# One DMA queue in place of two: whole 32 KB rows, and loads and stores in turn, in a contrast kernel

## The chip, the cores and the metric

The kernel runs on one core of a Trainium2 chip. The metric is the device time of one execution in microseconds, as the median of the runs. The profile's span, from the first to the last instruction, is a little shorter.

## The reference

The input is a batch of 16 images with 3 channels of 512 x 512 pixels in float32, 48 planes in all. Each plane gets its own mean, its contrast is raised by 1.5 around that mean, and the result is clipped to 0 and 1:

```python
x = np.random.rand(16, 3, 512, 512).astype(np.float32)   # factor = 1.5
mean = np.mean(x, axis=(2, 3), keepdims=True)
return np.clip(mean + factor * (x - mean), 0, 1).astype(np.float32)
```

So 50.33 MB are read and 50.33 MB are written, and no pixel of a plane can be finished before all of that plane has been read.

## The kernel before

A plane of 262144 pixels is laid over 32 partitions with rows of 8192 floats (32 KB). Four planes fill the 128 partitions and make one tile of 4 MB; there are 12 tiles. The tiles pass through `ring`, six buffers of 128 x 8192 floats, and are worked on in place. The program is written under a manual schedule: each engine runs its instructions in the order in which the code names them.

For each tile there are these steps:

- `load` (L74): a DMA on SyncE's queue brings the tile into buffer t % 6. Tiles 0 and 1 come singly, 2 and 3 in one DMA, 4 and 5 in one DMA; tiles 6 to 11 come singly, each once the store that held its buffer has landed.
- `add` (L89): ScalarE copies the tile onto itself and accumulates each partition's sum into `sums`.
- `shift_by` (L94): TensorE multiplies the sums with `blockw`, a matrix with blocks of 32 x 32 that hold (1 - factor) / pixels. The result in PSUM, `bias`, has for each partition the amount to be added after the scaling.
- `clip` (L78 and L82): VectorE multiplies by the factor and adds the bias, and then applies the maximum with 0 and the minimum with 1.
- `store` (L99): a DMA on ScalarE's queue writes the tile out.

Tile 0 is handled in pieces. VectorE sums its first 4352 columns (L108) while ScalarE sums the other 3840, and the clip and the store go in cuts of 1024, 2048 and 5120 columns, so the first pieces of the output leave early. In the loop over the later tiles the order on ScalarE is: the sum of tile t + 1, then the issue of the store of tile t. SyncE issues loads only, so its waits for free buffers hold back nothing but loads.

The two queues, q1 (SyncE's, loads) and q10 (ScalarE's, stores), both feed the same 16 DMA engines.

Of the kernel before, what the change touches and what calls it, by code (L numbers as in the profile page):

```python
# [1 line left out]

# [4 lines left out]


P = 128  # L10
ROW = 8192
BUFS = 6
CUTS = (0, 1024, 3072, ROW)
SUM = 4352


@with_exitstack
def kernel(
    ctx: ExitStack,
    tc: tile.TileContext,  # L20
    x: bass.AP,
    factor: float,
    out: bass.AP,
):

    nc = tc.nc
    f32 = mybir.dt.float32
    Alu = mybir.AluOpType  # L30
    Act = mybir.ActivationFunctionType

    B, C, H, W = x.shape
    n_img, n_pix = B * C, H * W
    ppi = n_pix // ROW
    per_tile = P // ppi
    n_tiles = n_img // per_tile
    assert ppi * ROW == n_pix and per_tile * n_tiles == n_img

    factor = float(factor)  # L40
    wconst = (1.0 - factor) / float(n_pix)

    x_f = x.rearrange("b c h w -> (b c h w)")
    out_f = out.rearrange("b c h w -> (b c h w)")

    def dram(ap, t, c0=0, c1=ROW):
        return bass.AP(tensor=ap.tensor, offset=t * P * ROW + c0, ap=[[ROW, P], [1, c1 - c0]])

    consts = ctx.enter_context(tc.tile_pool(name="consts", bufs=1))
    xpool = ctx.enter_context(tc.tile_pool(name="xpool", bufs=1))  # L50
    small = ctx.enter_context(tc.tile_pool(name="small", bufs=1))
    psum = ctx.enter_context(tc.tile_pool(name="psum", bufs=1, space=bass.MemoryType.PSUM))


    sums = small.tile([P, 2 * n_tiles], f32, name="sums")
    bias = psum.tile([P, n_tiles], f32, name="bias")

    blockw = consts.tile([P, P], f32, name="blockw")
    nc.gpsimd.memset(blockw, 0.0)  # L59
    for a in range(0, P, ppi):  # L60
        nc.gpsimd.memset(blockw[a : a + ppi, a : a + ppi], wconst)  # L61


    ring = xpool.tile([P, BUFS, ROW], f32, name="ring")

    def load(t, c0=0, c1=ROW, n=1):

        b = t % BUFS
        src = bass.AP(
            tensor=x_f.tensor,  # L70
            offset=t * P * ROW + c0,
            ap=[[ROW, P], [P * ROW, n], [1, c1 - c0]],
        )
        nc.sync.dma_start(out=ring[:, b : b + n, c0:c1], in_=src)  # L74

    def clip(t, c0, c1):
        part = ring[:, t % BUFS, c0:c1]
        nc.vector.tensor_scalar(  # L78
            out=part, in0=part, scalar1=factor, scalar2=bias[:, t : t + 1],
            op0=Alu.mult, op1=Alu.add,  # L80
        )
        nc.vector.tensor_scalar(  # L82
            out=part, in0=part, scalar1=0.0, scalar2=1.0, op0=Alu.max, op1=Alu.min
        )

    def add(t, c0=0):
        part = ring[:, t % BUFS, c0:ROW]
        own = sums[:, 2 * t : 2 * t + 1]
        nc.scalar.activation(out=part, in_=part, func=Act.Copy, accum_out=own)  # L89
        return own  # L90

    def shift_by(t, *parts):
        for k, part in enumerate(parts):
            nc.tensor.matmul(  # L94
                bias[:, t : t + 1], blockw, part, start=k == 0, stop=k == len(parts) - 1
            )

    def store(t, c0, c1):
        nc.scalar.dma_start(out=dram(out_f, t, c0, c1), in_=ring[:, t % BUFS, c0:c1])  # L99

    with tc.manual_schedule():
        load(0)
        load(1)
        load(2, n=2)
        load(4, n=2)

        rest = sums[:, 1:2]
        nc.vector.tensor_reduce(  # L108
            out=rest, in_=ring[:, 0, 0:SUM], axis=mybir.AxisListType.X, op=Alu.add
        )  # L110
        shift_by(0, add(0, SUM), rest)
        for c0, c1 in zip(CUTS[:-2], CUTS[1:-1]):
            clip(0, c0, c1)
            store(0, c0, c1)
        clip(0, CUTS[-2], ROW)
        own = add(1)
        store(0, CUTS[-2], ROW)
        load(BUFS)
        for t in range(1, n_tiles):
            shift_by(t, own)  # L120
            clip(t, 0, ROW)
            if t + 1 < n_tiles:
                own = add(t + 1)
            store(t, 0, ROW)
            if t + BUFS < n_tiles:
                load(t + BUFS)


# [1 line left out]
_INS = ['x', 'factor']  # L130
_OUTS = [((16, 3, 512, 512), 'float32')]

_NUMBERS = {'factor': 1.5}


# [26 lines left out]
```

## Time and profile before

| What | Value |
|---|---|
| Time, median of 3 runs | 239.14 us (238.86 to 239.28) |
| Span of the profiled execution | 237.8 us |
| Moved by DMA | 100.66 MB in 3712 packets, mean 423 GB/s |
| VectorE busy | 112.1 us (47%) |
| ScalarE busy | 82.9 us (35%) |
| TensorE busy | 7.6 us (3%) |
| Sum of a whole tile on ScalarE | 7.03 us |
| Clip of a whole tile on VectorE | 4.49 + 4.43 us |

The page of the profiled execution gives its span; an execution time of its own is not listed beside it, and the median lies 1.3 us above the span. The profile has forty slices of the span with the DMA engines' busy share and rate, the waits of each engine with what ended them, a list of DMA issues with the time from issue to landing, and a timeline. The time to landing counts from the start of the issuing instruction and contains the time for which the transfer stood behind others.

### The profile page before, as it was taken

Reading aid. Unit: us, or ns where it says so; the run is one execution under the profiler, and the core shown is the slowest. Engines: PE = TensorE matmul, PEld = TensorE weight load, DVE = VectorE, ACT = ScalarE, POOL = GpSimd, SP = SyncE. Lnnn points to the kernel's source line nnn. Section 1 sums busy time; section 2 is a strip of 40 time slices with the busy share of each in tenths; the row PEclk is TensorE's granted clock in tenths of the full one; section 3 lists DMA queues with packets and bytes.
Section 4 is the critical chain, followed back from the end, with each engine's and each line's share of the span. In section 5 each row is a group of like instructions: output and inputs, shape, how many; then the busy total and the mean of one; then the engine's idle time right before and its main releaser. Section 6 shows DMA issues by size and latency. Waiting matters only on the chain.

```text
span 237.8 us, 219 instructions
## 1 busy us (share of the span) xinstructions
PE 7.6 (3%) x26; PEld 6.5 (3%) x26; DVE 112.1 (47%) x29; ACT 82.9 (35%) x25; POOL 0.9 (0%) x9
## 2 busy tenths in 40 slices
PE   0010000000000000000000000000000000000000
PEld 0000000000000000000000000000000000000000
DVE  0078786009990039979407705902920950770000
ACT  2051900399000697380091083056038009100000
POOL 1000000000000000000000000000000000000000
DMA  7999999999999999999999999999999999999996
GB/s 265 441 441 442 401 471 429 391 413 430 457 441 435 413 408 430 435 435 441 441 441 441 441 435 435 402 419 430 435 441 441 441 441 441 441 430 413 413 430 259
DMA packets 3712, 100.66 MB, mean 423 GB/s; under 512 B 384, under 2 KB 384, under 8 KB 512
## 3 DMA queue, kind: packets, MB, share of 16 engines
q1 hardware_dynamic: 1696, 50.33, 49.6%
q10 hardware_dynamic: 2016, 50.33, 49.1%
HBM read 50.33 MB, written 50.33 MB: 423 GB/s over the span
## 4 chain that ended last, share of the span: by engine, by line
DMA 52%; another core or an unknown queue 15%; DVE 11%; issue 9%; PE 1%; ACT 1%; SPq 0%; ACTq 0%
DMA ring<-in_x_dram 33%; DMA out_dram<-ring 20%; DVE ring L78 6%; DVE ring L82 6%; PE bias L94 1%; ACT ring L89 1%; SPq L74 0%; ACTq L99 0%; ACTq L89 0%
## 5 line engine op out<-in xcount | busy, mean ns | idle before, releaser
L89 ACT ACTIVATE ring<-ring 128x8192 f32<-128x8192 f32 (+1 forms) x12 | 80.7, 6725 | 119.4 <-DMA ring<-in_x_dram 119.4
L78 DVE TENSOR_SCALAR ring<-ring,bias 128x8192 f32<-128x8192 f32 (+3 forms) x14 | 54.3, 3880 | 87.1 <-PE bias L94 87.1
L82 DVE TENSOR_SCALAR ring<-ring 128x8192 f32<-128x8192 f32 (+3 forms) x14 | 53.4, 3817 | 0.5
L94 PE MATMUL bias<-sums,blockw 128*128 128x1 f32 x26 | 7.6, 361 | 196.1 <-ACT ring L89 195.6
L94 PEld LDWEIGHTS bias<-sums,blockw 128*128 128x128 f32 x26 | 6.5, 311 | 197.1 <-ACT ring L89 179.9
L108 DVE TENSOR_REDUCE sums<-ring 128x1 f32<-128x4352 f32 x1 | 4.7, 4686 | 13.0 <-DMA ring<-in_x_dram 13.0
L89 ACT ACTIVATION_READ_ACCUMULATOR ring<-ring 128x1 f32 x12 | 2.2, 186 | 0.0
L89 ACT ACT_TABLE_LOAD x1 | 1.3, 1283 | 0.7 <-PEq L143 0.7
L61 POOL MEMSET blockw<- 32x32 f32 x4 | 0.5, 116 | 0.2
L59 POOL MEMSET blockw<- 128x128 f32 x1 | 0.2, 205 | 0.3 <-POOLq L143 0.3
L143 POOL MEMSET const-bfloat16-1.0<- 128x1 bf16 x1 | 0.1, 111 | 0.0
L143 POOL MEMSET const-uint8-127<- 128x1 uint8 x1 | 0.1, 111 | 0.0
L143 POOL MEMSET const-float32-1.0<- 128x1 f32 x1 | 0.1, 108 | 0.0
L143 POOL MEMSET const-float32-0.0<- 128x1 f32 x1 | 0.1, 103 | 0.2 <-issue 0.2
## 6 DMA issues: line engine op xcount, KB each, us to landing
out_dram<-ring ACTq DMA_DIRECT2D x11, 4096.0 KB, 44.2
ring<-in_x_dram SPq DMA_DIRECT2D x8, 4096.0 KB, 33.3
ring<-in_x_dram SPq DMA_DIRECT2D x2, 8192.0 KB, 60.6
out_dram<-ring ACTq DMA_DIRECT2D x1, 2560.0 KB, 37.5
out_dram<-ring ACTq DMA_DIRECT2D x1, 1024.0 KB, 25.9
out_dram<-ring ACTq DMA_DIRECT2D x1, 512.0 KB, 16.1
```

The lines of the kernel that those rows point to most:

```text
L59: nc.gpsimd.memset(blockw, 0.0)
L61: nc.gpsimd.memset(blockw[a : a + ppi, a : a + ppi], wconst)
L78: nc.vector.tensor_scalar(out=part, in0=part, scalar1=factor, scalar2=bias[:, t : t + 1], op0=Alu.mult, op1=Alu.add,)
L82: nc.vector.tensor_scalar(out=part, in0=part, scalar1=0.0, scalar2=1.0, op0=Alu.max, op1=Alu.min)
L89: nc.scalar.activation(out=part, in_=part, func=Act.Copy, accum_out=own)
L94: nc.tensor.matmul(bias[:, t : t + 1], blockw, part, start=k == 0, stop=k == len(parts) - 1)
L108: nc.vector.tensor_reduce(out=rest, in_=ring[:, 0, 0:SUM], axis=mybir.AxisListType.X, op=Alu.add)
L143: nc = _bacc.Bacc("TRN2", target_bir_lowering=False, num_devices=1)
```

## The change

All loads and stores go on SyncE's queue, each a whole tile with rows of 32 KB. The paired loads and the cuts of tile 0 are gone: tile 0 is summed by ScalarE alone, clipped whole and stored whole, as the others are. On SyncE the order of issue is: loads 0 to 5, stores 0 and 1, load 6, store 2, load 7, store 3, and so on to load 11, and then stores 7 to 11. A load of tile t + 5 is issued behind store t, and it waits for store t - 1 to land, since that store frees its buffer. ScalarE issues no DMA any more.

```diff
-    def load(t, c0=0, c1=ROW, n=1):
-
-        b = t % BUFS
-        src = bass.AP(
-            tensor=x_f.tensor,
-            offset=t * P * ROW + c0,
-            ap=[[ROW, P], [P * ROW, n], [1, c1 - c0]],
-        )
-        nc.sync.dma_start(out=ring[:, b : b + n, c0:c1], in_=src)
+    def load(t):
+        nc.sync.dma_start(out=ring[:, t % BUFS, :], in_=dram(x_f, t))
...
+    def store(t):
+        nc.sync.dma_start(out=dram(out_f, t), in_=ring[:, t % BUFS, :])
...
-    def store(t, c0, c1):
-        nc.scalar.dma_start(out=dram(out_f, t, c0, c1), in_=ring[:, t % BUFS, c0:c1])
...
     with tc.manual_schedule():
-        load(0)
-        load(1)
-        load(2, n=2)
-        load(4, n=2)
+        for t in range(BUFS):
+            load(t)
 
-        rest = sums[:, 1:2]
-        nc.vector.tensor_reduce(
-            out=rest, in_=ring[:, 0, 0:SUM], axis=mybir.AxisListType.X, op=Alu.add
-        )
-        shift_by(0, add(0, SUM), rest)
-        for c0, c1 in zip(CUTS[:-2], CUTS[1:-1]):
-            clip(0, c0, c1)
-            store(0, c0, c1)
-        clip(0, CUTS[-2], ROW)
-        own = add(1)
-        store(0, CUTS[-2], ROW)
-        load(BUFS)
-        for t in range(1, n_tiles):
-            shift_by(t, own)
-            clip(t, 0, ROW)
-            if t + 1 < n_tiles:
-                own = add(t + 1)
-            store(t, 0, ROW)
-            if t + BUFS < n_tiles:
-                load(t + BUFS)
+
+        for t in range(n_tiles):
+            shift_by(t, add(t))
+            clip(t)
+            store(t)
+            if 0 <= t - 1 < n_tiles - BUFS:
+                load(t - 1 + BUFS)
```

The helper `add` is written with a range of columns, and `clip` without one; the operations of `add`, `shift_by` and `clip` on a whole tile are the same as before.

More of the change, by code (lines that the diff above doesn't have):

```diff
@@ L12 @@
 BUFS = 6
-CUTS = (0, 1024, 3072, ROW)
-SUM = 4352
 @with_exitstack
@@ L37 @@
     n_tiles = n_img // per_tile
-    assert ppi * ROW == n_pix and per_tile * n_tiles == n_img
+    assert ppi * ROW == n_pix and per_tile * n_tiles == n_img and n_tiles > BUFS
     factor = float(factor)
@@ L44, with dram @@
     out_f = out.rearrange("b c h w -> (b c h w)")
-    def dram(ap, t, c0=0, c1=ROW):
-        return bass.AP(tensor=ap.tensor, offset=t * P * ROW + c0, ap=[[ROW, P], [1, c1 - c0]])
+    def dram(ap, t):
+        return bass.AP(tensor=ap.tensor, offset=t * P * ROW, ap=[[ROW, P], [1, ROW]])
     consts = ctx.enter_context(tc.tile_pool(name="consts", bufs=1))
@@ L64, with add, shift_by, clip @@
     ring = xpool.tile([P, BUFS, ROW], f32, name="ring")
-    def load(t, c0=0, c1=ROW, n=1):
-        b = t % BUFS
-        src = bass.AP(
-            tensor=x_f.tensor,
-            offset=t * P * ROW + c0,
-            ap=[[ROW, P], [P * ROW, n], [1, c1 - c0]],
-        )
-        nc.sync.dma_start(out=ring[:, b : b + n, c0:c1], in_=src)
-    def clip(t, c0, c1):
-        part = ring[:, t % BUFS, c0:c1]
+    def load(t):
+        nc.sync.dma_start(out=ring[:, t % BUFS, :], in_=dram(x_f, t))
+    def store(t):
+        nc.sync.dma_start(out=dram(out_f, t), in_=ring[:, t % BUFS, :])
+    def add(t, c0=0, c1=ROW):
+        part = ring[:, t % BUFS, c0:c1]
+        k = 2 * t + (c0 > 0)
+        own = sums[:, k : k + 1]
+        nc.scalar.activation(out=part, in_=part, func=Act.Copy, accum_out=own)
+        return own
+    def shift_by(t, *parts):
+        for k, part in enumerate(parts):
+            nc.tensor.matmul(
+                bias[:, t : t + 1], blockw, part, start=k == 0, stop=k == len(parts) - 1
+            )
+    def clip(t):
+        part = ring[:, t % BUFS, :]
         nc.vector.tensor_scalar(
@@ L84, in clip @@
         )
[L86 to L95, printed above, removed]
-            )
-    def store(t, c0, c1):
-        nc.scalar.dma_start(out=dram(out_f, t, c0, c1), in_=ring[:, t % BUFS, c0:c1])
-    with tc.manual_schedule():
-        load(0)
-        load(1)
-        load(2, n=2)
-        load(4, n=2)
-        rest = sums[:, 1:2]
-        nc.vector.tensor_reduce(
-            out=rest, in_=ring[:, 0, 0:SUM], axis=mybir.AxisListType.X, op=Alu.add
-        )
-        shift_by(0, add(0, SUM), rest)
-        for c0, c1 in zip(CUTS[:-2], CUTS[1:-1]):
-            clip(0, c0, c1)
-            store(0, c0, c1)
-        clip(0, CUTS[-2], ROW)
-        own = add(1)
-        store(0, CUTS[-2], ROW)
-        load(BUFS)
-        for t in range(1, n_tiles):
-            shift_by(t, own)
-            clip(t, 0, ROW)
-            if t + 1 < n_tiles:
-                own = add(t + 1)
-            store(t, 0, ROW)
-            if t + BUFS < n_tiles:
-                load(t + BUFS)
+    with tc.manual_schedule():
+        for t in range(BUFS):
[6 more added lines that the diff above has]
+                load(t - 1 + BUFS)
 _INS = ['x', 'factor']
```

## The prediction

> **What bounds the kernel now.** I read the busy shares first, then the DMA row, then who waits for whom, then the landings of single transfers, which give the price of a tile. The page's parts 1 to 3, in part:
>
> ```profile
> PE 7.6 (3%) x26; PEld 6.5 (3%) x26; DVE 112.1 (47%) x29; ACT 82.9 (35%) x25; POOL 0.9 (0%) x9
> ...
> DMA  7999999999999999999999999999999999999996
> ...
> q1 hardware_dynamic: 1696, 50.33, 49.6%
> q10 hardware_dynamic: 2016, 50.33, 49.1%
> ```
>
> No engine is busy for half the span; the 16 DMA engines are full in every slice but the first and the last. The two queues share them: 49.6 + 49.1 = 98.7%. The windows of four stages (columns: stretch, its length, busy us of each engine with its instruction count, clock, DMA share, GB/s):
>
> ```profile
> 5.00:22.00 17.00, 1.14 (x4) 1.00 (x4) 8.24 (x5) 3.50 (x2) 0.00 (x0) 1.00 1.00 434
> 22.00:85.00 63.00, 1.76 (x6) 1.51 (x6) 32.62 (x9) 26.93 (x7) 0.00 (x0) 1.00 1.00 427
> 60.00:190.00 130.00, 4.51 (x16) 3.82 (x16) 70.25 (x17) 49.75 (x14) 0.00 (x0) 1.00 1.00 433
> 197.00:235.00 38.00, 0.59 (x2) 0.50 (x2) 8.92 (x2) 6.07 (x2) 0.00 (x0) 1.00 1.00 433
> ```
>
> Loads alone (434), both directions (433) and stores alone (433) run at one rate, so the mix does not matter to it. Only 22 to 85 us lies lower, at 427; it holds store 0, cut in pieces, and the two paired loads.
>
> The waits say that the compute follows the loads:
>
> ```profile
> ACT ring L89 <- DMA ring<-in_x_dram: 119.4, 10, 19.6
> DVE ring L78 <- PE bias L94: 87.1, 10, 15.9
> SPq L74 <- DMA out_dram<-ring: 157.5, 8, 33.3
> ```
>
> ScalarE stands 119.4 us for loads, VectorE 87.1 us for the sums behind them, and SyncE 157.5 us for stores to free a buffer. The timeline gives the pitch (start, duration, engine, line, operation):
>
> ```profile
> 118.33 7.03 ACT L89 ACTIVATE ring<-ring 128x8192 f32<-128x8192 f32 x1 [12.34 <-DMA ring<-in_x_dram]
> ...
> 195.94 7.03 ACT L89 ACTIVATE ring<-ring 128x8192 f32<-128x8192 f32 x1 [12.26 <-DMA ring<-in_x_dram]
> ```
>
> Four loads and four stores pass between these two starts: (195.94 - 118.33) / 8 = 9.70 us for a 4 MB transfer. From issue times and times to landing, load 0 lands at 0.74 + 12.2 = 12.94, load 1 at 1.12 + 21.5 = 22.62: 9.68 later, alone on one queue. The stores 7 to 11 land at 137.86 + 60.4 = 198.26, then 207.96, 217.61, 227.30 and 212.73 + 24.3 = 237.03: 9.69 each. I take **9.69 us a tile**, between 9.67 and 9.71.
>
> **What could be gained at all.** 24 transfers end to end behind the first landing give 12.94 + 23 x 9.69 = 235.81 us. Before has its last landing at 237.03, so 1.22 us are lost on the way, and 0.8 us follow to the span's end (237.8). Where they are lost: when store 1 lands (45.65 + 39.2 = 84.85), six loads, two stores and (84.85 - 79.3) / (98.87 - 79.3) = 0.28 of load 6 have passed, 7.28 tiles after the first, which should have taken to 12.94 + 70.5 = 83.5. So about 1.3 us are gone by 85 us. The windows agree: 63 us x (433 - 427) / 433 = 0.9 us in 22 to 85. After 85 us nothing is lost.
>
> **The change part by part.**
> Whole rows and single loads: store 0 loses its pieces of 1024, 2048 and 5120 columns, and the loads of two tiles become single ones. The stretch in which these are in flight loses 0.9 to 1.3 us. Bounds for what comes back: none of it, if the loss belongs to the first meeting of loads and stores in general, and all 1.22. I take all, since stages with whole rows alone lose nothing measurable, mixed or not.
>
> One queue in place of two: the transfers now pass in the order of issue: loads 0 to 5, stores 0 and 1, load 6, store 2, load 7, and so on to load 11, then stores 7 to 11. The bytes stay the same. What is new is a change of direction inside one queue, 13 times (once after load 5, once before and once after each of the loads 6 to 11). The trace of before has no such step. Bounds: nothing (load behind load 9.68, store behind store 9.69, the same as in the mixed stage, so a boundary between transfers costs nothing), and a full restart of an idle queue, 12.2 - 9.69 = 2.51 us, the start-up that load 0 shows. A gain is excluded: no spacing of two landings lies below 9.65, and times to landing are given to 0.1 us. I take nothing: it is nearest to the boundaries between queued transfers, where the next one already stands in the queue. The Trainium skill speaks against it: "DMA: Bandwidth & Descriptors", section "Anatomy of one DMA — SWDGE (gpsimd) path", gives each DMA a fixed cost of about 2.0 us, mostly the receipt of the last write, for transfers of another path. If this were paid 13 times it would add an estimated 26 us; the 9.68 us between two queued loads show that queued transfers do not pay it here.
>
> A new order of waits on SyncE: SyncE now waits for VectorE's clip of a tile before each store, and for an old store before each load, and all later transfers stand behind that wait. Where would the queue run dry? The first store is the first risk. Before, its first piece went at 19.89. Now load 0 lands at 12.94, the whole sum is 7.03 + 0.19, the matmuls some 0.85 with their gaps, the clip 4.49 + 4.43: store 0 is ready at about 30. But loads 1 to 5 hold the DMA engines until 12.94 + 5 x 9.69 = 61.4, so this lies under 31 us of loads. Without that cover the later start would cost 10 us. Load 6 waits for store 0's landing at 61.4 + 9.69 = 71.1; store 1, issued at about 39.5, still has 9.69 us to move, against 0.4 us of issue and at most 2.51 us of start-up: 6.8 us to spare. That is the tightest place. At each later landing two transfers stand queued (load 6 and store 2 when store 1 lands). Behind the waiting load stands store 2, ready since about 49 and sent at 71.5, while its turn in the queue is at 12.94 + 8 x 9.69 = 90.5. The last tile: load 11 is the 19th transfer, landing at 12.94 + 18 x 9.69 = 187.4 where it was 195.9; 17 us later its store is ready, at 204.4, and its turn comes at 12.94 + 22 x 9.69 = 226.1. Each is hidden: cost nothing.
>
> VectorE's reduction of 4.69 us (L108), the small clips and one matmul go; ScalarE's first sum grows from 3.40 to 7.03 us. ScalarE issues no stores any more (14 x 0.34 us), SyncE 14 more steps in all. Six single issues of some 0.35 us are 2.1 us, against 2.02 before, under load 0. None of it is on the path: at the pitch of 19.4 us a tile ScalarE needs 7.2 and VectorE 8.95.
>
> **Sum.** 237.03 - 1.22 = 235.8 for the last landing, span 236.6. The page lists no execution time of its own for this run beside the span of 237.8; the median of the runs shown lies 1.3 us over it, so the forecast is 239.14 - 1.22 = 237.9 us. The tile price of 9.67 to 9.71 moves this by 0.46 either way, the runs lie 0.2 around their median: 237.2 to 238.6 for this case.
>
> **The rivals.**
> - **The loss comes back**: the 1.2 us belong to loads and stores meeting for the first time, or to one DMA engine lagging, and appear again around 61 us. For it: the windows show the place and not the cause. Against it: 130 us of mixed traffic at 433. Time 239.1 (238.6 to 239.7).
> - **Direction changes leave a gap** (the other side): every change in the one queue stops the DMA engines for a moment, which the two queues covered for each other. From 1.22 / 13 = 0.094 us a change the gain is gone; from (1.22 + 0.48) / 13 = 0.13 us it is slower by over 0.2%. For it: nothing in the trace shows a load and a store behind each other in one queue. Against it: boundaries of one direction cost nothing. At 0.2 us, 239.14 - 1.22 + 2.6 = 240.5; with the full 2.51 us it is 270.5.
> - **SyncE's waits empty the queue**: a ready store stands behind a load that waits. On the same page and in the same section the Trainium skill says that waits are held by the issuing sequencer before dispatch; the SPq row above shows it. It would need a landing more than 6.8 us later than worked out. If six loads each paid a start-up of 2.51 us, the time would be 237.9 + 15.1 = 253.
>
> That the change does not do what it says is excluded: its instructions stand in this order on SyncE's queue, each with the waits used above and a few on transfers that lie eight places back.
>
> **How the numbers follow.** Forecast 0.62; the loss comes back 0.17, of which 0.15 within 0.2% (0.48 us, about what a measurement of this kernel can tell from no change) and 0.02 a little faster; gaps at direction changes 0.17; an empty queue 0.04. So faster 0.64, same 0.15, slower 0.21. The range goes from 237.2 to 240.3: it holds the forecast, the second case and gaps up to (240.3 - 237.9) / 13 = 0.18 us, which is about a third of the third case.
>
> **What would show it.** Right: DMA slices full from the second on, all at 430 GB/s or more; the first store landing near 71, the last load near 187, then five stores 9.69 us apart, the last landing near 235.8. Gaps would show as stretches below 430 GB/s between 60 and 190 us and as a pitch of loads over 19.4 us; an empty queue as a slice with a DMA digit under 9. The forecast is wrong if the last landing lies past 237.

## The result, and the profile after

The changed kernel takes **241.51 us** (median of 6 runs, 240.35 to 242.39) against 238.89 us for the kernel before (238.81 to 239.28) in the same comparison: a ratio over the runs of 1.0099, with a 95% interval of 1.0085 to 1.0113. It is slower by 1%, where 0.5% faster was forecast. Its runs also differ by 2 us among themselves, those of before by 0.5.

The page of the profiled execution after (span 239.8 us, time 241.61 us), parts 1 to 3:

```profile
PE 7.0 (3%) x24; PEld 6.0 (2%) x24; DVE 107.0 (45%) x24; ACT 86.8 (36%) x25; POOL 0.9 (0%) x9
...
DMA  7999999999899999999999999999999999999992
...
q1 hardware_dynamic: 3456, 100.66, 98.0%
```

No engine has become the bound, and the one queue keeps the DMA engines at 98.0% of the span. Two slices differ from before: one near 60 us has a digit of 8, and the last has 2. The windows say where the rate is lower (columns as before, GB/s last):

```profile
5.00:50.00 45.00, 2.31 (x8) 2.00 (x8) 26.82 (x7) 28.49 (x8) 0.00 (x0) 1.00 1.01 435
50.00:66.00 16.00, 0.59 (x2) 0.50 (x2) 15.17 (x4) 10.93 (x3) 0.00 (x0) 1.00 0.99 403
66.00:195.00 129.00, 3.51 (x12) 2.99 (x12) 56.12 (x13) 43.36 (x13) 0.00 (x0) 1.00 1.01 433
197.00:235.00 38.00, 0.59 (x2) 0.50 (x2) 8.92 (x2) 0.69 (x2) 0.00 (x0) 1.00 1.01 438
```

The stretch in which the loads end and the stores begin falls to 403. The mean over the alternating stretch is still 433, which is 4 MB every 9.69 us. It is a mean over 16 engines, though, and a tile has landed only when the last of them has finished its part; that landing is what ScalarE's timeline shows (start of the sum of tiles 4 to 11):

```profile
51.85 7.03 ACT L70 ACTIVATE ring<-ring 128x8192 f32<-128x8192 f32 x1 [2.59 <-DMA ring<-in_x_dram]
62.19 7.03 ACT L70 ACTIVATE ring<-ring 128x8192 f32<-128x8192 f32 x1 [3.21 <-DMA ring<-in_x_dram]
91.58 7.03 ACT L70 ACTIVATE ring<-ring 128x8192 f32<-128x8192 f32 x1 [22.27 <-DMA ring<-in_x_dram]
111.08 7.03 ACT L70 ACTIVATE ring<-ring 128x8192 f32<-128x8192 f32 x1 [12.38 <-DMA ring<-in_x_dram]
130.76 7.03 ACT L70 ACTIVATE ring<-ring 128x8192 f32<-128x8192 f32 x1 [12.56 <-DMA ring<-in_x_dram]
150.66 7.03 ACT L70 ACTIVATE ring<-ring 128x8192 f32<-128x8192 f32 x1 [12.77 <-DMA ring<-in_x_dram]
171.20 7.03 ACT L70 ACTIVATE ring<-ring 128x8192 f32<-128x8192 f32 x1 [13.42 <-DMA ring<-in_x_dram]
190.56 7.03 ACT L70 ACTIVATE ring<-ring 128x8192 f32<-128x8192 f32 x1 [12.24 <-DMA ring<-in_x_dram]
```

Tile 5, the last before the first store, comes 10.34 us after tile 4, where 9.70 is usual: 0.64 late. From tile 5 to tile 11 there are 13 transfers, 126.0 us at 9.69, and they take 128.37: **2.4 us late**. The pitch of the loads is 19.50, 19.68, 19.90, 20.54 and 19.36, where 19.38 was due. The last five stores lose nothing: load 11 lands at 190.54 (160.44 + 30.1), the last store at 239.04 (207.34 + 31.7), 9.70 us each.

Which engines lose this time can be read from the events of the trace. It keeps sixteen completions of each transfer, which no printed view lists; they are taken here as one for each DMA engine, and the sum starts right behind the last (load 11: last completion at 190.54 us, sum at 190.56). Load 4 is completed from 51.30 to 51.83 us and load 5 from 61.73 to 62.16, so around the first store all sixteen come 0.6 to 0.7 us late together. Load 11 is completed by fourteen from 187.61 to 188.24 us, 126 us behind their load 5 and so in time, and by the other two only at 189.36 and 190.54. The first loss is one of all engines, the later 2.4 us are the loss of one, with a second 1.3 late. At the end such engines work alone, at a share of 0.10, less than two of 16:

```profile
235.00:239.80 4.80, 0.00 (x0) 0.00 (x0) 0.00 (x0) 0.00 (x0) 0.00 (x0) 1.00 0.10 41
```

SyncE's waits answer the rival of the empty queue:

```profile
SPq L61 <- DMA out_dram<-ring: 115.8, 6, 32.1
SPq L64 <- DVE ring L85: 80.2, 5, 26.1
```

They are long, but a landing frees the next load with one or two transfers still in the queue (store 0 lands at 29.86 + 42.0 = 71.9, store 1 at 39.49 + 42.3 = 81.8). The alternating stretch at 433 GB/s leaves no room for an empty queue. The slice near 60 us, with its digit of 8, is the sign that the prediction gave for one, but stores 0 and 1 had been issued by then, at 29.86 and 39.49 us.

### The profile page after: what moved, and what is told of

Its sections match the earlier page's. It is cut to its first block, busy times and chain, and to the rows that moved or that the text cites. A ratio compares the mean times of both kernels' runs of the same rounds, so it can differ in the third digit from the quotient of the medians.

```text
span 239.8 us, 194 instructions
## 1 busy us (share of the span) xinstructions
PE 7.0 (3%) x24; PEld 6.0 (2%) x24; DVE 107.0 (45%) x24; ACT 86.8 (36%) x25; POOL 0.9 (0%) x9
## 4 chain that ended last, share of the span: by engine, by line
DMA 68%; DVE 11%; ACT 6%; PE 1%; SPq 0%; issue 0%; ACTq 0%
DMA out_dram<-ring 50%; DMA ring<-in_x_dram 18%; ACT ring L70 6%; DVE ring L81 6%; DVE ring L85 6%; PE bias L75 1%; SPq L61 0%; ACTq L130 0%; SPq L64 0%
## 5 line engine op out<-in xcount | busy, mean ns | idle before, releaser
L70 ACT ACTIVATE ring<-ring 128x8192 f32<-128x8192 f32 x12 | 84.4, 7030 | 110.2 <-DMA ring<-in_x_dram 110.2
L81 DVE TENSOR_SCALAR ring<-ring,bias 128x8192 f32<-128x8192 f32 x12 | 53.9, 4492 | 99.9 <-PE bias L75 99.9
L85 DVE TENSOR_SCALAR ring<-ring 128x8192 f32<-128x8192 f32 x12 | 53.1, 4427 | 0.4
L75 PE MATMUL bias<-sums,blockw 128*128 128x1 f32 x24 | 7.0, 360 | 191.3 <-ACT ring L70 182.3
L75 PEld LDWEIGHTS bias<-sums,blockw 128*128 128x128 f32 x24 | 6.0, 310 | 192.2 <-ACT ring L70 172.0
```

The lines of the kernel that those rows point to most:

```text
L75: nc.tensor.matmul(bias[:, t : t + 1], blockw, part, start=k == 0, stop=k == len(parts) - 1)
L81: nc.vector.tensor_scalar(out=part, in0=part, scalar1=factor, scalar2=bias[:, t : t + 1], op0=Alu.mult, op1=Alu.add,)
L85: nc.vector.tensor_scalar(out=part, in0=part, scalar1=0.0, scalar2=1.0, op0=Alu.max, op1=Alu.min)
```

## The experiments

In what follows a **turn** is a place in the one queue where a load is followed by a store. The changed kernel has seven, one behind load 5 (the first turn) and six behind the loads 6 to 11. Each time stands beside the median of the kernel before in the same comparison, which was 238.99 to 239.08 throughout (238.89 for the change itself).

**Fewer and more turns, with one queue.** Three kernels change nothing but the order of issue. Six and six:

```diff
             store(t)
-            if 0 <= t - 1 < n_tiles - BUFS:
-                load(t - 1 + BUFS)
+            if t == BUFS - 1:
+                for n in range(BUFS, n_tiles):
+                    load(n)
```

> One queue, in the order six loads, six stores, six loads, six stores: two places where a load is followed by a store, in place of seven. Theory A at 0.46 us a place: 241.5 - 5 x 0.46 = 239.2; if the first place costs 0.8 and each later one 0.4, 241.5 - 5 x 0.4 = 239.5. Theory B (time lost with mixed traffic, not with changes): 241.5. If all loss sits in the first place: 241.5.

Three and three:

```diff
             store(t)
-            if 0 <= t - 1 < n_tiles - BUFS:
-                load(t - 1 + BUFS)
+            if t in (2, 5):
+                for n in range(t + 4, t + 7):
+                    load(n)
```

> One queue, six loads, then three stores and three loads in turn, then the last stores: three places where a load is followed by a store. Theory A: 241.5 - 4 x 0.4 to 4 x 0.46 = 239.7 to 239.9, between the order of six and the changed kernel. Theory B: 241.5.

Turns from the fourth load on:

```diff
-        for t in range(BUFS):
+        for t in range(4):
             load(t)
...
             store(t)
-            if 0 <= t - 1 < n_tiles - BUFS:
-                load(t - 1 + BUFS)
+            if t + 4 < n_tiles:
+                load(t + 4)
```

> One queue, but loads and stores alternate from the fourth load on: nine places where a load is followed by a store, the first at 42 us in place of 61. Theory A: 241.5 + 2 x 0.4 to 0.46 = 242.3 to 242.4, and the stretch of about 0.8 us of loss moves to the end of load 3, so the sum of tile 3 starts late by some 0.6 us while tiles 0 to 2 keep their 9.7 us. Theory B with a loss at a fixed time: the loss stays at 54 to 66 us, 241.5.

| Order | Turns | Time, us | Ratio to before, interval |
|---|---|---|---|
| six and six | 2 | 239.19 | 1.0007 (0.9999 to 1.0016) |
| three and three | 3 | 239.39 | 1.0017 (1.0007 to 1.0027) |
| the change | 7 | 241.51 | 1.0099 (1.0085 to 1.0113) |
| from the fourth load | 9 | 242.18 | 1.0124 (1.0108 to 1.0140) |

Theory A holds within 0.4 us each time; from two turns to nine it is 2.99 / 7 = 0.43 us a turn. It is not one price, though: the second and third cost little, the four from three to seven cost 0.53 each, and the 0.67 us from seven to nine are less than the 2 us by which runs of the change differ. With the turns grow the opposite changes, a store followed by a load (one, two, six and eight), so these orders do not say which of the two changes beside a load costs the time. The timeline of the order of six and six (sums of tiles 4, 5, 6 and 11):

```profile
51.83 7.03 ACT L70 ACTIVATE ring<-ring 128x8192 f32<-128x8192 f32 x1 [2.60 <-DMA ring<-in_x_dram]
62.07 7.03 ACT L70 ACTIVATE ring<-ring 128x8192 f32<-128x8192 f32 x1 [3.12 <-DMA ring<-in_x_dram]
...
129.95 7.03 ACT L70 ACTIVATE ring<-ring 128x8192 f32<-128x8192 f32 x1 [60.75 <-DMA ring<-in_x_dram]
...
178.52 7.03 ACT L70 ACTIVATE ring<-ring 128x8192 f32<-128x8192 f32 x1 [2.60 <-DMA ring<-in_x_dram]
```

The first turn still costs 10.24 - 9.70 = 0.54 us; the 12 transfers from tile 5 to 11 take 116.45, 9.70 each, with no loss. In the order with early turns the first turn moves with its load (sums of tiles 2 and 3, 10.59 us apart, 0.89 late):

```profile
32.42 7.03 ACT L70 ACTIVATE ring<-ring 128x8192 f32<-128x8192 f32 x1 [2.59 <-DMA ring<-in_x_dram]
43.01 7.03 ACT L70 ACTIVATE ring<-ring 128x8192 f32<-128x8192 f32 x1 [3.48 <-DMA ring<-in_x_dram]
```

So this loss belongs to the turn, not to a time.

**Two queues with whole rows.** The other half of the change alone: rows and loads as after, queues as before.

```diff
-        load(0)
-        load(1)
-        load(2, n=2)
-        load(4, n=2)
+        for t in range(BUFS):
+            load(t)
...
+        own = add(0)
+        for t in range(n_tiles):
             shift_by(t, own)
             clip(t, 0, ROW)
             if t + 1 < n_tiles:
                 own = add(t + 1)
             store(t, 0, ROW)
```

> Whole rows and single loads as in the changed kernel, but the stores stay on ScalarE's queue, as before. Theory A (a load followed by a store in one queue holds the DMA engines, 3.2 us over seven such places): no such place here, so the 1.2 us of the cut rows and paired loads come back as gain, 237.7 us, or 238.5 if the 0.8 us of the first meeting of loads and stores stay. Theory B (the DMA engines lose time once stores begin, and single engines lag more and more in mixed traffic, whatever queue it is in): 241, as the changed kernel. Theory C (the gain was never there, and one queue costs what the change lost): 238.9, as before.

It took 244.08 us (ratio 1.0211, 1.0194 to 1.0227), which none of the theories had. Whole rows and single loads bring no gain; with two queues they lose 5 us, and the move to one queue then wins 2.6 of these back. The Trainium skill ("DMA: Bandwidth & Descriptors", section "Issuing engines are not separate DMA queues") says that issuing from several engines only saves issue time, which is usually small beside the transfer; here the same transfers on two queues or one differ by 2.6 us, in an order that differs as well. Which of the two parts loses the 5 us was asked next.

```diff
-        load(2, n=2)
-        load(4, n=2)
+        for t in range(2, BUFS):
+            load(t)
```

> The kernel before with tiles 2 to 5 loaded singly; the cuts of tile 0 and the two queues stay. It parts the two halves of what the kernel with two queues and whole rows (244.1) lacks. If the cuts keep the two queues in step: 239.0, as before. If the paired loads do: 244.1. If each does a part: about 241.5.

The mirror keeps `load(2, n=2)` and `load(4, n=2)` and handles tile 0 whole:

> The kernel before with tile 0 summed, clipped and stored whole; the paired loads and the two queues stay. The mirror of the kernel with cuts and single loads. If the cuts matter: 244.1. If the paired loads matter: 239.0. If each does a part: about 241.5. By the prediction's term for short rows it would be 1.2 us faster than before, 237.8.

Cuts with single loads: **251.98 us** (1.0558, 1.0522 to 1.0595). Paired loads with whole rows: 239.89 us (1.0039, 1.0027 to 1.0051). None of the expected values came for the first of these, and for the mirror the paired loads come nearest. So the paired loads win 4.2 us without the cuts and 13 with them; the cuts win 0.9 beside the pairs and lose 7.9 without them (251.98 against 244.08), where the prediction charged cuts and pairs together 1.2. The slow one shows how a loss appears while the mean rate hardly falls. Its windows:

```profile
85.00:195.00 110.00, 2.93 (x10) 2.50 (x10) 44.59 (x10) 37.90 (x11) 0.00 (x0) 1.00 1.01 427
235.00:238.00 3.00, 0.00 (x0) 0.00 (x0) 0.00 (x0) 0.00 (x0) 0.00 (x0) 1.00 0.81 350
238.00:250.00 12.00, 0.00 (x0) 0.00 (x0) 0.00 (x0) 0.00 (x0) 0.00 (x0) 1.00 0.06 27
```

From 238 to 250 us the mean is 27 GB/s and the share 0.06: 433 / 16 = 27, one DMA engine of 16 that finishes its part alone. The completions of the last store agree: fourteen from 238.58 to 238.73 us, the fifteenth at 239.66, the last at 249.49, some 10 us behind. Why it falls behind there, and not with paired loads, stays open.

**The stores of the turns without their writes to memory.**

```diff
     def store(t):
-        nc.sync.dma_start(out=dram(out_f, t), in_=ring[:, t % BUFS, :])
+        buf = ring[:, t % BUFS, :]
+        nc.sync.dma_start(out=dram(out_f, t) if t > BUFS else buf, in_=buf)
```

> The changed kernel, in which stores 0 to 6 are left out: each is a transfer of the same 4 MB from its buffer onto itself, at the same place in the queue with the same waits; only stores 7 to 11 write the output. Theory A (the change of direction inside a queue itself holds the engines): the loads still start their sums 0.64 us late at the first place and 0.1 to 1.2 us late at the later ones, 241.5. Theory D (a load's reads of the memory are held where writes to the memory follow): all of it is gone up to the end of load 11, sums of loads 6 to 11 every 19.4 us, and only the one place before store 7 stays: 238.4 to 239.2. If such copies move at another rate, the pitch shows it and the time is read from the first place alone.

It took 239.40 us (239.17 to 239.69; ratio 1.0015, 1.0006 to 1.0023). The sums of tiles 4, 5, 6 and 11:

```profile
51.86 7.03 ACT L71 ACTIVATE ring<-ring 128x8192 f32<-128x8192 f32 x1 [2.60 <-DMA ring<-in_x_dram]
62.13 7.03 ACT L71 ACTIVATE ring<-ring 128x8192 f32<-128x8192 f32 x1 [3.15 <-DMA ring<-in_x_dram]
91.28 7.03 ACT L71 ACTIVATE ring<-ring 128x8192 f32<-128x8192 f32 x1 [22.03 <-DMA ring<-in_x_dram]
...
188.40 7.03 ACT L71 ACTIVATE ring<-ring 128x8192 f32<-128x8192 f32 x1 [12.31 <-DMA ring<-in_x_dram]
```

From tile 5 to 11 it is 126.27 us, 0.3 over 13 x 9.69, where the changed kernel loses 2.4: the six later turns cost almost nothing once the stores of five of them do not write to the memory (the sixth, in front of store 7, still does). The completions of load 11 lie within 0.61 us (187.77 to 188.38): no engine is late. The first turn, 10.27 between tiles 4 and 5, costs 0.57 as before, which theory D did not have. They are two losses: the later one needs stores that write to the memory, as theory D says (that it is the loads' reads which are held is not shown), and the first one does not.

**A small store ahead of the first turn**, in the order of six and six:

```diff
+        load(0)
+        load(1)
+        nc.sync.dma_start(
+            out=bass.AP(tensor=out_f.tensor, offset=(n_tiles - 1) * P * ROW, ap=[[ROW, P], [1, P]]),
+            in_=blockw,
+        )
+        for t in range(2, BUFS):
+            load(t)
```

> The order of six loads and six stores (239.2), with a store of 64 KB (the block matrix, into rows of tile 11 that its own store overwrites later) put into the queue behind load 1. It asks what the 0.8 us at the first place belong to. If to the first change of direction in the queue, whatever its size: they move from load 5 to load 1 (the sum of tile 1 starts some 0.6 us late, that of tile 5 in time), 239.2. If to the first large store: they stay at load 5, 239.4. If a small store takes them off: 238.5, faster than before by 0.2%.

239.57 us (1.0025, 1.0015 to 1.0035). The loss stays behind load 5 (10.25 us between the sums of tiles 4 and 5); the small store costs no more than 0.14 at its own place. So the first loss comes with the first large transfer out of a buffer, be it to the memory or, as in the kernel with copies, back into the buffer; its cause stays open.

**The same turns at other addresses.** `dram` takes tile 5 * t % 12, or 7 * t % 12, in place of t:

```diff
-        return bass.AP(tensor=ap.tensor, offset=t * P * ROW, ap=[[ROW, P], [1, ROW]])
+        return bass.AP(tensor=ap.tensor, offset=(5 * t % n_tiles) * P * ROW, ap=[[ROW, P], [1, ROW]])
```

> The changed kernel with the tiles taken in the order 0, 5, 10, 3, 8, 1, 6, 11, 4, 9, 2, 7: the queue, its turns and its waits are the same, only the distance in memory between a load and the stores beside it is another. Theory D1 (the later loss, which is gone where the stores do not write to the memory, comes from which addresses are read and written at once): the pitch of loads 6 to 11 and the time move by 1 us or more, down to 239.2 where no addresses collide. Theory D2 (reads of a lagging DMA engine lose against the writes of the others, whatever the addresses): 241.5, within the 1 us by which runs of the changed kernel differ.

> As the order by fives, but 0, 7, 2, 9, 4, 11, 6, 1, 8, 3, 10, 5, so that a load lies one tile below or above where the order by fives has it. Theory D1: another time than 241.5, and not that of the order by fives. Theory D2: 241.5 again.

> The kernel with two queues, single loads and whole rows (244.1), with the tiles in the order by fives. Theory D1: the 5 us that it loses against before are another sum, in the best case gone (239). Theory D2, or a loss that comes from the phase between the two queues: 244.1.

241.65 us (240.06 to 242.12), 241.31 us (240.68 to 242.48), and with two queues 243.91 us (242.49 to 244.68; 244.08 without the new order). All three as before the reordering: D1 falls, and the distance between the addresses read and written is not the cause. The two traces of the one queue suggest why its runs differ by 2 us, namely by how far an engine falls behind: in the order by fives, where the profiled execution is the fastest of its six (240.06 us), the completions of load 11 lie within 1.05 us (187.97 to 189.02), and in the order by sevens (242.48 us) they are spread over 3.88 (187.55 to 191.43).

**A lag given beforehand.** One more transfer behind load 1, in the changed kernel and in the order of six and six:

```diff
+    extra = small.tile([17, LAG], f32, name="extra")       # LAG = 512
...
         for t in range(BUFS):
             load(t)
+            if t == 1:
+                few = bass.AP(tensor=x_f.tensor, offset=0, ap=[[ROW, 17], [1, LAG]])
+                nc.sync.dma_start(out=extra, in_=few)
```

> The changed kernel with one more transfer behind load 1: 17 pieces of 2 KB into a tile of their own, on 17 partitions, which no computation uses. It is meant to fall on one DMA engine or few, and to make them lag by up to 17 x 2 KB, by the rate of one engine (433 / 16 = 27 GB/s) 1.3 us, long before the first turn. Theory D2 with a lag that feeds itself (a lagging engine reads while the others write, and loses more the more it lags): later than 241.5 + 1.3 = 242.8, the pitch of the loads 6 to 11 up by more than the 0.1 to 1.2 us of the changed kernel. Theory E (each turn costs an engine its own bit, whatever its lag): 241.5 to 242.8.

> The control: the same 17 pieces in the order of six loads and six stores (239.2), which has one turn after the first place. Both theories: the 1.3 us of work on the lagging engine alone, 239.2 + 1.3 = 240.5; a little more if that one turn feeds the lag; 239.2 if the pieces spread over all engines.

243.29 us (243.01 to 243.55) and 241.32 us (240.93 to 241.68). In the changed order, the sums of tiles 1, 2, 4, 5, 6 and 11:

```profile
22.83 7.03 ACT L73 ACTIVATE ring<-ring 128x8192 f32<-128x8192 f32 x1 [2.56 <-DMA ring<-in_x_dram]
33.97 7.03 ACT L73 ACTIVATE ring<-ring 128x8192 f32<-128x8192 f32 x1 [4.01 <-DMA ring<-in_x_dram]
...
53.40 7.03 ACT L73 ACTIVATE ring<-ring 128x8192 f32<-128x8192 f32 x1 [2.59 <-DMA ring<-in_x_dram]
64.45 7.03 ACT L73 ACTIVATE ring<-ring 128x8192 f32<-128x8192 f32 x1 [3.93 <-DMA ring<-in_x_dram]
94.04 7.03 ACT L73 ACTIVATE ring<-ring 128x8192 f32<-128x8192 f32 x1 [22.47 <-DMA ring<-in_x_dram]
...
192.28 7.03 ACT L73 ACTIVATE ring<-ring 128x8192 f32<-128x8192 f32 x1 [12.44 <-DMA ring<-in_x_dram]
```

The lag is there: tile 2 comes 11.14 us after tile 1, 1.4 late, and every later tile keeps it. (The Trainium skill, "DMA: Bandwidth & Descriptors", section "Why a DMA increments its semaphore by 16 and not by 1", has the number of partitions here decide over how many DMA engines a transfer is spread; by its rule that is one for 17. The 1.4 us for 17 x 2 KB agree.) The first turn costs the lagging engine more: 11.05 - 9.70 = 1.35 us, and 1.41 in the control (64.50 - 53.39 = 11.11), which is why the control came 0.8 us above the expected 240.5. But from tile 5 to 11 it is 127.83 us, 1.8 over the due 126.0, no more than the 2.4 without a lag, and the two kernels differ by 1.97 us, where those without the lag differ by 2.32. By its time alone (over 242.8) the run would speak for D2, but the growth from load 6 on that D2 asked for is not there. So a lag given beforehand does not grow faster at the later turns, as far as one trace each and runs 2 us apart can say, and E stands, apart from 0.5 us above its range, which the first turn explains.

## Why the prediction was wrong, step by step

**The base of the sum.** The forecast took 1.3 us for what lies around the span (239.14 - 237.8). The runs show 1.8 for both kernels (241.61 - 239.8 after; runs of before with 239.11 us and a span of 237.3). By that, the profiled execution of before took an estimated 239.6 us, 0.5 more than its usual run, and what could be gained was about 0.7 us, not 1.22. This cost 0.5.

**Whole rows and single loads.** "I take all" was wrong: the loss in 22 to 85 us was put on short rows and paired loads, while whole rows in one queue lose 0.54 to 0.89 us at the first turn in every order without an added lag, wherever that turn lies. So far the rival of the first meeting of loads and stores was right, in place and at about half its size. Whether the loss of the kernel before has the same cause is not shown; its trace has a late engine as well, which that rival also named (of the sixteen completions of the last store fifteen have come by 236.21 us, and the last comes at 236.99). The cuts and pairs that went were worth something with two queues: 239.89 without the cuts, 251.98 without the pairs. No stage of the profile of before could show that, since the kernel never ran without them. The term missed 0.64 us.

**One queue, 13 changes of direction, taken at nothing.** This is the step that failed: the row taken for it, a boundary between two queued transfers of one direction, is not a change of direction. The runs show 2.4 us from load 5 to load 11, gone with six loads and six stores in turn (239.19 us), and almost gone where the stores between do not write to the memory (239.40). The rival named the place and the deciding price, 0.094 us a change; all 3.0 us over 13 changes are 0.23, just past its example of 0.2 (240.5). Its picture was another, every change stopping the engines for a moment: the trace has one stop of all sixteen, and then one engine that falls behind. The mixed stage at 433 GB/s, read as "the mix does not matter", was a mean over 16 engines, and the landing waits for the slowest. The fixed cost of about 2.0 us a transfer that the Trainium skill gives for another path ("DMA: Bandwidth & Descriptors", section "Anatomy of one DMA — SWDGE (gpsimd) path"), paid 13 times, would be an estimated 26 us; the 3.0 us here are far below it.

Together: 0.5 + 0.6 + 2.4 = 3.5, and 237.9 + 3.5 = 241.4, against 241.51.

**What was right.** SyncE's new waits cost nothing; the first store landed at 71.9 (71.1 was given), the late first store and the longer first sum are hidden, the last five stores run at 9.70 us, and TensorE, VectorE and ScalarE do not bound. "An empty queue" did not happen.

The cause is settled so far: the 2.4 us are lost where single loads and stores that write to the memory alternate in one queue, in the landing of one or two DMA engines; they follow neither the addresses nor an earlier lag. Which of the two changes beside a load costs them, and why one engine loses time and the others do not, is open, as is the 0.6 us that all engines lose at the first turn. No order tried beats the kernel before: six and six equals it.

## What to carry to other kernels

When a kernel is bound by DMA, a mean rate near the ceiling hides a late engine: read the pitch of the landings, since each waits for the slowest of 16. In one queue, keep loads together and stores together as far as the buffers allow; here six of each cost 2.3 us less than turns after every tile. And one profiled execution can be some tenths of a microsecond longer than the usual run: set its span against the spans of several runs before what it loses is counted as a gain.

## What the runs showed of the hardware that was not expected

- A single DMA engine can fall some 10 us behind the other 15: with cuts and single loads in two queues, the last store's fifteenth completion came at 239.66 us and its last at 249.49.
- Of two losses that look alike in the start of a sum, the first holds all sixteen engines for 0.6 to 0.7 us, and the later one leaves fourteen of them in time.
- Loading tiles 2 to 5 in pairs of 8 MB is worth 4.2 us (239.89 against 244.08) when loads and stores have a queue each; why is not shown.
- 4 MB copied from a buffer onto itself pass at the same pitch as a store to memory (13 transfers, loads included, in 126.27 us), and cost almost nothing at the later turns.
